# A pool of their own for the tiles of two matmul operands, in a two-layer decoder trunk

## The chip, the cores and the metric

One core of a Trainium2 chip runs the whole kernel. A time is that of one execution on the device, in microseconds (us); the runs shown are three, and their median is what a version is judged by. A profiled execution is a further one, with the hardware profiler on, and has a time of its own.

## The reference

The kernel computes two decoder layers on a residual stream x of 512 tokens by 1024 features, in float32. Each layer is a mixer and then a squared-ReLU MLP, with an RMS norm before each:

```python
for layer in range(DEPTH):                     # DEPTH = 2
    h = rmsnorm(x, norm_gains[layer, 0])
    if layer % 2 == 0:
        x = x + stick_breaking_mixer(h, ...)   # 16 heads of 64; w_qkv 1024x3072, w_o 1024x1024
    else:
        x = x + hgrn2_mixer(h, ...)            # 8 heads of 128; w_in 1024x4096, w_o 1024x1024
    h = rmsnorm(x, norm_gains[layer, 1])
    a = relu(h @ w1)                           # w1 1024x4096
    x = x + (a * a) @ w2                       # w2 4096x1024
```

The stick-breaking mixer is causal attention whose weights are products of sigmoids in place of a softmax, with normalised queries and keys. The HGRN2 mixer is a gated linear recurrence, done in blocks. Nearly all of the arithmetic is in the five matrix products with weights.

## The kernel before

The residual stream lies transposed in `xT`, eight tiles of 128 features by 512 tokens. Every product with weights is done in three passes, to keep the precision of float32 with the faster fp32r matmul: an operand is split into a high part, rounded to fp32r, and a low part, the rest; the product is then high x high + low x high + high x low. So each product of one 128x128 block of weights is a triple of matmuls.

**Weights.** They come in slabs (`slab_halves`, line 247): 512 KB twice by DMA into `wr`, then ScalarE copies to `wh` (line 263) and VectorE subtracts to `wl` (line 264). Two slabs are held, one in use and the next in preparation. A slab has 1024 rows by 256 columns, or 512 by 512 in the two projections.

**Activations.** `act_pair` (line 335) takes two tiles of 128 by 512, a high and a low one. With tag P these are the normalised inputs `xh` and `xl` of a sub-layer (`Norm.split`, line 354), 16 tiles for the eight feature blocks. With tag Q they are the second moving operand: `hh` and `hl` of the MLP's hidden layer (line 677), or `oh` and `ol` of a mixer's output (`split_out`, line 338), 16 tiles too.

**Two forms of product.** In `gemm_w` (line 312) a block of the slab is stationary and an activation tile moves, all 512 columns of it; eight triples make one output tile. It is used for w1 with P moving, for w2 and the projections with Q moving, and for q and f of the recurrence with P moving. In `gemm_x` (line 324) it is the other way round: a 128x128 block of P is stationary, and 256 columns of the slab move; q, k, v of the attention and i, g of the recurrence are made so. The very last output tile of the kernel is done in two halves of 256 tokens each (line 686).

**Order.** TensorE's instructions are in an order written out by hand: `line.run` (line 130) interleaves the long products with the short tasks of the attention heads, the recurrence and the norms, by costs and due times in `COST` and `LAG`. The other engines' order comes from the scheduler. An MLP is four rounds; each makes eight hidden tiles with w1 and adds eight partial outputs of w2 to `xT`.

**Places in memory.** Tiles come from pools: `cp` for constants and `xT`, `wp` for the slabs, `ap` for everything else, `pp` in PSUM. The function `sb` (line 90) takes all tiles of `ap`; a tile's tag says which buffers it shares, and `BUFS` how many of them there are. The pools lie in SBUF in the order in which they are opened, from the lowest address up, behind 16 KiB that are reserved; within a pool the tags lie in the order of their first use. `cp` takes 22.4 KiB of each partition, `wp` 44 KiB (two `wh` and two `wl` of 8 KiB, three `wr` of 4), and `ap` the rest. In `ap`, the tags in their order and in KiB are AT 6, sq 4, R4 16, ss 0.25, P 32, st 0.75, sn 4, mqk 0.25, mx and rx 0.1, B 8, qT 26, X5 10, Q 32, bc 2, tf 0.1. The last address in use is 144 bytes under the end of the 224 KiB.

Of the kernel before, what the change touches and what calls it, by code (L numbers as in the profile page):

```python
# [58 lines left out]
def trunk(  # L59
# [18 lines left out]
    PSUM = bass.MemoryType.PSUM  # L78
    cp = ctx.enter_context(tc.tile_pool(name="cp", bufs=1))
    wp = ctx.enter_context(tc.tile_pool(name="wp", bufs=2))  # L80
    ap = ctx.enter_context(tc.tile_pool(name="ap", bufs=2))
    pp = ctx.enter_context(tc.tile_pool(name="pp", bufs=2, space=PSUM))

    BUFS = {
        "P": 16, "Q": 16, "X5": 2, "R4": 4, "B": 2, "qT": 13, "sn": 2, "AT": 3, "sq": 2, "bc": 1,
        "st": 6, "mx": 2, "rx": 2, "ss": 2, "mqk": 2, "tf": 4,
    }
    PB = {"mm": 2, "z": 2, "tr": 3, "av": 1}

    def sb(tag, shape=(P, S), dt=F32, name=None):  # L90
        return ap.tile(list(shape), dt, tag=tag, bufs=BUFS[tag], name=name or tag)

    def ps(tag, shape=(P, S), name=None):
        return pp.tile(list(shape), F32, tag=tag, bufs=PB[tag], name=name or f"ps_{tag}")
# [72 lines left out]
    nc.scalar.copy(ones_r, ones)  # L167

    rows = sb("AT", (40, P), name="rows")
    nc.sync.dma_start(out=rows[0:32, :], in_=norm_gains.rearrange("l j (k p) -> (l j k) p", p=P))  # L170
    nc.sync.dma_start(out=rows[32:40, :], in_=hg_lb_logits.rearrange("a (k p) -> (a k) p", p=P))
    warm = sb("sq", (P, 1), name="warm")
    nc.scalar.activation(out=warm, in_=ones[:, 0:1], func=AF.Sigmoid)
    cols = cp.tile([P, 40], F32, name="cols")
# [25 lines left out]
    def late_constants():  # L200
        nc.vector.tensor_mul(gqk, gq, gk)
        masks_i = sb("R4", (P, level_masks.shape[1]), I32, name="masks_i")
        nc.gpsimd.dma_start(out=masks_i, in_=level_masks)
        nc.gpsimd.tensor_copy(pairs, masks_i[:, 0 : P // 2])
        nc.gpsimd.tensor_copy(masks, masks_i[:, P // 2 :])

        lg = cols[:, 32:40]
        e0 = sb("st", (P, 32), name="e0")[:, :KT]  # L210
        e1 = sb("st", (P, 32), name="e1")[:, :KT]
        nc.vector.tensor_sub(lb, lg, lg)
        nc.scalar.activation(out=e0, in_=lb, func=AF.Sigmoid)
        nc.scalar.activation(out=e1, in_=lb, func=AF.Sigmoid, scale=-1.0)
        nc.vector.reciprocal(out=e1, in_=e1)
        nc.vector.tensor_mul(e0, e0, e1)
        nc.vector.reciprocal(out=e1, in_=e0)
        nc.vector.tensor_mul(e0, e0, e1)
        nc.vector.tensor_sub(lb, e0, e0)
        nc.vector.tensor_scalar(  # L220
            out=oml, in0=lb, scalar1=-1.0, scalar2=1.0, op0=ALU.mult, op1=ALU.add
        )
# [863 lines left out]
```

## Time and profile before

| | us |
|---|---|
| median of 3 runs | 1322.77 |
| lowest, highest | 1321.46, 1326.64 |
| profiled execution, its own time | 1325.41 |
| its span, first to last instruction | 1323.7 |
| TensorE busy (PE) | 1300.2 |
| VectorE busy (DVE) | 798.7 |
| ScalarE busy (ACT) | 446.0 |
| GpSimd busy (POOL) | 80.0 |

In the profile, PE is a matmul and PEld the load of its stationary operand, which goes beside it. Matmuls are pipelined: the end of one lies after the start of the next, and a busy PE is not a PE at its peak. The distance from start to start is what one costs. The mean granted clock of TensorE was 0.996 of its full speed. In the rows, an operand list such as `ps_mm<-xh,wh` has the moving operand first and the stationary one second; buffer numbers are left out.

### The profile page before, as it was taken

The page shows a single profiled execution, that of the slowest core. Times are in us where ns is not written, and L with a number is a line of the kernel's source. Part 1 is how long each engine was busy: PE and PEld are TensorE (multiplying, and loading weights), DVE is VectorE, ACT ScalarE, POOL GpSimd, SP SyncE. Part 2 cuts the span into 40 slices and gives each one's busy share as a digit, 9 for nine tenths or more (in the row PEclk, how much of TensorE's full clock was granted, in tenths as well). Part 3 has the DMA queues.
Part 4 walks back from the last instruction along what each step waited for, and adds up shares of the span by engine and source line. Part 5 has one row for each costly group of instructions (what it writes and reads, how often), then busy time and mean ns, then how long its engine had stood idle before and what let it go on. Part 6 is the DMA issues. An engine that isn't in the chain of part 4 may idle for free.

```text
span 1323.7 us, 17619 instructions
## 1 busy us (share of the span) xinstructions
PE 1300.2 (98%) x6993; PEld 1104.2 (83%) x6993; DVE 798.7 (60%) x1534; ACT 446.0 (34%) x756; POOL 80.0 (6%) x139
## 2 busy tenths in 40 slices
PE   7999999999999999999999999999999999999998
PEld 7989898778888888888888888888888888888887
DVE  5787687867535435345578888797764353453441
ACT  5554454544212222123333333342432221221221
POOL 0100000000000000000013222232000000000000
PEclk8999999999999999999999999999999999999999
DMA  5312121113333333333321222221333333333331
GB/s 178 108 33 65 33 68 61 49 48 96 96 96 96 96 96 96 96 96 96 96 89 47 88 64 65 64 65 64 96 96 96 96 96 96 95 96 94 97 96 48
DMA packets 110657, 110.64 MB, mean 84 GB/s; under 512 B 3848, under 2 KB 106416, under 8 KB 110576
## 3 DMA queue, kind: packets, MB, share of 16 engines
q1 hardware_dynamic: 110496, 109.22, 26.7%
q8 instruction: 55, 0.90, 0.3%
q0 software_dynamic: 80, 0.31, 0.1%
q14 instruction: 26, 0.21, 0.0%
HBM read 107.41 MB, written 2.10 MB: 83 GB/s over the span
## 4 chain that ended last, share of the span: by engine, by line
PE 84%; DVE 10%; POOL 2%; issue 2%; ACT 1%; SPq 1%; DMA 1%; DVEq 0%; POOLq 0%; ACTq 0%
PE ps_mm L151 70%; PE po L151 3%; PE ps_z L151 3%; POOL tot L812 2%; DVE sc L845 2%; PE ps_s L151 2%; DVE wl L264 2%; PE pa L155 1%; PE z L151 1%; DVE qr L826 1%; PE po_h L151 1%; PE ps_tr L151 1%; DVE sn L591 1%; DVE X L863 1%; DVE X L867 1%
## 5 line engine op out<-in xcount | busy, mean ns | idle before, releaser
L263 ACT CAST wh<-wr 128x1024 fp32r<-128x1024 f32 x198 | 199.8, 1051 | 399.8 <-PE ps_mm L151 367.8
L264 DVE TENSOR_TENSOR wl<-wr,wh 128x1024 fp32r<-128x1024 f32 x198 | 237.7, 1230 | 17.6 <-ACT wh L263 16.8
L151 PE MATMUL ps_mm<-xh,wh 128*128 128x512 f32 x592 | 232.1, 392 | 0.0
L151 PE MATMUL ps_mm<-xh,wl 128*128 128x512 f32 x592 | 230.5, 389 | 0.0
L151 PE MATMUL ps_mm<-xl,wh 128*128 128x512 f32 x592 | 230.5, 389 | 0.0
L151 PE MATMUL ps_mm<-hh,wh 128*128 128x512 f32 (+1 forms) x520 | 204.1, 393 | 0.0
L151 PE MATMUL ps_mm<-hh,wl 128*128 128x512 f32 (+1 forms) x520 | 203.6, 392 | 0.0
L151 PE MATMUL ps_mm<-hl,wh 128*128 128x512 f32 (+1 forms) x520 | 203.5, 391 | 0.0
L151 PE MATMUL ps_mm<-wh,xh 128*128 128x256 f32 x592 | 173.6, 293 | 0.0
L695 DVE TENSOR_TENSOR xT<-xT,ps_mm 128x512 f32<-128x512 f32 x63 | 43.4, 688 | 213.2 <-PE ps_mm L151 213.2
L151 PE MATMUL ps_mm<-wl,xh 128*128 128x256 f32 x592 | 167.8, 283 | 3.1 <-DVE wl L459 3.1
L151 PE MATMUL ps_mm<-wh,xl 128*128 128x256 f32 x592 | 167.6, 283 | 0.0
L151 PEld LDWEIGHTS ps_mm<-xh,wl 128*128 128x128 f32 x592 | 111.1, 188 | 23.2
L151 PEld LDWEIGHTS ps_mm<-xh,wh 128*128 128x128 f32 x592 | 111.2, 188 | 22.7
L151 PEld LDWEIGHTS ps_mm<-xl,wh 128*128 128x128 f32 x592 | 111.2, 188 | 22.5
L151 PEld LDWEIGHTS ps_mm<-wh,xh 128*128 128x128 f32 x592 | 113.5, 192 | 4.2 <-issue 3.6
L151 PEld LDWEIGHTS ps_mm<-wl,xh 128*128 128x128 f32 x592 | 113.6, 192 | 3.9 <-DVE wl L459 3.3
L151 PEld LDWEIGHTS ps_mm<-hh,wl 128*128 128x128 f32 x520 | 97.6, 188 | 22.9
L151 PEld LDWEIGHTS ps_mm<-hl,wh 128*128 128x128 f32 x520 | 97.7, 188 | 22.7
L151 PEld LDWEIGHTS ps_mm<-hh,wh 128*128 128x128 f32 x520 | 97.7, 188 | 22.6
L672 DVE SCALAR_TENSOR_TENSOR u<-ps_mm,R 128x512 f32<-128x512 f32 x60 | 41.5, 692 | 123.1 <-PE ps_mm L151 123.1
L151 PEld LDWEIGHTS ps_mm<-wh,xl 128*128 128x128 f32 x592 | 113.5, 192 | 0.0
(213 smaller groups left out, 1653.6 us busy)
## 6 DMA issues: line engine op xcount, KB each, us to landing
wr<-in_mlp_w_dram SPq DMA_DIRECT2D x128, 512.0 KB, 3.7
wr<-in_hg_w_in_dram SPq DMA_DIRECT2D x32, 512.0 KB, 3.8
wr<-in_sb_w_qkv_dram SPq DMA_DIRECT2D x22, 512.0 KB, 3.5
wr<-in_sb_w_o_dram SPq DMA_DIRECT2D x8, 512.0 KB, 3.9
wr<-in_hg_w_o_dram SPq DMA_DIRECT2D x8, 512.0 KB, 3.7
xin<-in_x_dram SPq DMA_DIRECT2D x8, 256.0 KB, 5.3
out_dram<-o SPq DMA_DIRECT2D x7, 256.0 KB, 2.3
wr<-in_sb_w_qkv_dram SPq DMA_DIRECT2D x4, 256.0 KB, 5.5
```

Source lines behind the costliest of these rows:

```text
L151: nc.tensor.matmul(o, lhsT=lhsT, rhs=rhs, start=start, stop=stop, **kw)
L155: nc.tensor.transpose(o, in_, ident)
L263: nc.scalar.copy(hi[:, c, :], raw)
L264: nc.vector.tensor_tensor(out=lo[:, c, :], in0=raw, in1=f(hi[:, c, :]), op=ALU.subtract)
L591: nc.vector.tensor_tensor_scan(out=rev, data0=rev, data1=later[:, S - W :][:, ::-1], initial=1.0, op0=ALU.mult, op1=ALU.max,)
L672: nc.vector.scalar_tensor_tensor(out=u, in0=p, scalar=0.0, in1=norm.R, op0=ALU.max, op1=ALU.mult)
L695: nc.vector.tensor_add(xT[m], xT[m], p)
L812: nc.gpsimd.tensor_tensor(out=tots[H][:, :, None], in0=t0, in1=t1, op=ALU.mult)
L826: nc.vector.tensor_tensor(out=q1, in0=q1, in1=t0.to_broadcast([P, S // (2 * H), H]), op=ALU.mult)
L845: nc.vector.copy_predicated(out=o, mask=mask.rearrange("p (g w) -> p g w", g=g)[:, None].to_broadcast([P, 2, g, w]), data=data.rearrange(" ...
L863: nc.vector.tensor_tensor(out=o, in0=qv[:, :, :, part * H : part * H + w], in1=tv[:, :, :, part - 1, None].to_broadcast([P, TT, g, w]), op ...
L867: nc.vector.tensor_tensor(out=C, in0=B[:, :, :, H:], in1=tv[:, :, :, 1, None].to_broadcast([P, TT, g, wc]), op=ALU.mult,)
```

## The change

A pool `gp` is opened between the slabs' pool and `ap`. Tiles with the tags P and Q come from it, each with its 16 buffers as before; all others stay in `ap`.

```diff
     cp = ctx.enter_context(tc.tile_pool(name="cp", bufs=1))
     wp = ctx.enter_context(tc.tile_pool(name="wp", bufs=2))
+    gp = ctx.enter_context(tc.tile_pool(name="gp", bufs=16))
     ap = ctx.enter_context(tc.tile_pool(name="ap", bufs=2))
...
     def sb(tag, shape=(P, S), dt=F32, name=None):
-        return ap.tile(list(shape), dt, tag=tag, bufs=BUFS[tag], name=name or tag)
+        pool = gp if tag in "PQ" else ap
+        return pool.tile(list(shape), dt, tag=tag, bufs=BUFS[tag], name=name or tag)
```

No other tag is a part of the text "PQ", so no other tile is moved to `gp`. The tiles of `ap` that lay behind P or Q, or before them, get other addresses too.

## Rows read from the trace of the kernel before

**Rows 1.** Page, part 1: busy us, share of the span, instructions of each engine.
```profile
PE 1300.2 (98%) x6993; PEld 1104.2 (83%) x6993; DVE 798.7 (60%) x1534; ACT 446.0 (34%) x756; POOL 80.0 (6%) x139
```
**Rows 2.** Page, part 4: the chain that ended last, by engine, by line.
```profile
PE 84%; DVE 10%; POOL 2%; issue 2%; ACT 1%; SPq 1%; DMA 1%; DVEq 0%; POOLq 0%; ACTq 0%
PE ps_mm L151 70%; PE po L151 3%; PE ps_z L151 3%; POOL tot L812 2%; DVE sc L845 2%; PE ps_s L151 2%; DVE wl L264 2%; PE pa L155 1%; PE z L151 1%; DVE qr L826 1%; PE po_h L151 1%; PE ps_tr L151 1%; DVE sn L591 1%; DVE X L863 1%; DVE X L867 1%
```
**Rows 3.** The same chain in order of time: start us, us, what.
```profile
321.86 342.41 PE ps_mm L151 x1488
...
973.96 306.71 PE ps_mm L151 x1335
```
**Rows 4.** Tiles xh, hh, oh on TensorE, one stretch each: duration ns, first and last start.
```profile
L151 PE MATMUL ps_mm<-xh,wh x64: 389/389/393, 399.1 to 442.0; 128*128 128x512 f32 x64
...
L151 PE MATMUL ps_mm<-hh,wh x64: 392/394/398, 442.7 to 486.8; 128*128 128x512 f32 x64
...
L151 PE MATMUL ps_mm<-oh,wl x32: 392/395/398, 287.5 to 309.2; 128*128 128x512 f32 x32
```
**Rows 5.** Timeline of TensorE, two short stretches: start us, us, instruction.
```profile
520.11 0.39 PE L151 MATMUL ps_mm<-xh,wh 128*128 128x512 f32 x1
520.34 0.39 PE L151 MATMUL ps_mm<-xl,wh 128*128 128x512 f32 x1
520.56 0.39 PE L151 MATMUL ps_mm<-xh,wl 128*128 128x512 f32 x1
...
521.47 0.39 PE L151 MATMUL ps_mm<-xh,wh 128*128 128x512 f32 x1
...
553.15 0.39 PE L151 MATMUL ps_mm<-hh,wl 128*128 128x512 f32 x1
553.38 0.40 PE L151 MATMUL ps_mm<-hh,wh 128*128 128x512 f32 x1
553.62 0.39 PE L151 MATMUL ps_mm<-hl,wh 128*128 128x512 f32 x1
553.85 0.40 PE L151 MATMUL ps_mm<-hh,wl 128*128 128x512 f32 x1
...
554.55 0.39 PE L151 MATMUL ps_mm<-hh,wl 128*128 128x512 f32 x1
...
553.15 0.19 PEld L151 LDWEIGHTS ps_mm<-hh,wh 128*128 128x128 f32 x1
553.38 0.19 PEld L151 LDWEIGHTS ps_mm<-hl,wh 128*128 128x128 f32 x1
```
**Rows 6.** Windows, w1 and w2: busy us of PE, PEld, DVE, ACT, POOL, PEclk, DMA.
```profile
400.00:442.00 42.00, 42.00 (x187) 34.76 (x187) 21.88 (x30) 11.23 (x15) 0.00 (x0) 1.00 0.33 101
443.00:487.40 44.40, 44.40 (x192) 35.73 (x191) 15.86 (x18) 8.17 (x9) 0.00 (x0) 1.00 0.30 95
```
**Rows 7.** Instruction groups by line, one of each three: count | busy us, mean ns.
```profile
L151 PE MATMUL ps_mm<-xh,wh 128*128 128x512 f32 x592 | 232.1, 392 | 0.0
...
L151 PE MATMUL ps_mm<-hh,wh 128*128 128x512 f32 (+1 forms) x520 | 204.1, 393 | 0.0
...
L151 PE MATMUL ps_mm<-wh,xh 128*128 128x256 f32 x592 | 173.6, 293 | 0.0
...
L151 PE MATMUL ps_mm<-ol,wh 128*128 128x512 f32 x128 | 50.9, 398 | 0.0
...
L151 PE MATMUL ps_z<-xh,wh 128*128 128x512 f32 x48 | 19.0, 396 | 0.0
```
**Rows 8.** 256 columns moving: tile wl at the start, then the timeline's end.
```profile
L151 PE MATMUL ps_tr<-wl,xh x32: 283/283/283, 29.5 to 40.7; 128*128 128x256 f32 x32
...
1313.13 0.29 PE L151 MATMUL ps_mm<-hh,wh 128*128 128x256 f32 x1
...
1313.86 0.28 PE L151 MATMUL ps_mm<-hh,wh 128*128 128x256 f32 x1
```
**Rows 9.** Instruction groups by line: matmuls with other moving tiles that get new places.
```profile
L151 PE MATMUL po<-at,V 128*64 128x128 f32 x320 | 48.9, 284 | 1.2 <-DVE at L610 1.2
...
L151 PE MATMUL ps_s<-X,kk 128*128 128x196 f32 (+1 forms) x192 | 40.9, 342 | 7.7 <-DVE sc L845 6.7 <-DVE sc L888 0.9
...
L151 PE MATMUL z<-kst,qh 128*128 128x256 f32 (+1 forms) x64 | 23.5, 368 | 3.2 <-ACT sg L589 3.2
```
**Rows 10.** Tiles hl and xT on VectorE: duration ns least, median, most.
```profile
L679 DVE TENSOR_TENSOR hl<-a,hh x64: 691/693/695, 326.2 to 1275.2; 128x512 fp32r<-128x512 f32 x64
...
L695 DVE TENSOR_TENSOR xT<-xT,ps_mm x63: 686/689/690, 360.1 to 1313.3; 128x512 f32<-128x512 f32 x63
```

## The prediction

> **What bounds the kernel now.** I read the busy shares first [rows 1]: TensorE is busy for 98% of the span, VectorE for 60%, ScalarE for 34%. Then the chain of waits by engine and line [rows 2]: 84% of it is TensorE, and 70% of the span is one line, the matmuls into `ps_mm`. In order of time [rows 3] this chain has two pieces of 342.41 and 306.71 us with nothing but such matmuls in them, 1488 and 1335 in a row. No other engine and no DMA ends a wait there. What the kernel takes in these stretches is a number of matmuls times the spacing from the start of one to the start of the next, so I looked at the spacing.
>
> It is not the same everywhere, and this is the finding on which all else rests. All long matmuls have 512 columns, a 128x128 stationary block of a slab (`wh` or `wl`), and one of two kinds of moving operand: tag P (`xh`, `xl`: w1, and q and f of the recurrence) or tag Q (`hh`, `hl`: w2; `oh`, `ol`: the projections). With P moving, 64 triples start from 399.1 to 442.0 us: 42.9/63/3 = 227.0 ns each [rows 4]. With Q moving, 64 triples start from 442.7 to 486.8 us: 44.1/63/3 = 233.3 ns [rows 4]. The timeline has the same at close range [rows 5]: seven starts with P from 520.11 to 521.47 are 1.36/6 = 226.7 ns apart, seven with Q from 553.15 to 554.55 are 1.40/6 = 233.3. The starts with P are 0.22 or 0.23 us apart, those with Q 0.23 and 0.24 in turn. The projection, which reads Q against slabs of another row length, has 32 triples from 287.5 to 309.2 us [rows 4]: 21.7/31/3 = 233.3. So the spacing goes with the tag, not with the slab's layout. Nor does it go with the load around it: in the w1 stretch VectorE is busy 21.88 us of 42.00 and the DMAs move 101 GB/s, in the w2 stretch 15.86 of 44.40 and 95, with a granted clock of 1.00 (2.4 GHz) in both [rows 6]. The less loaded stretch is the slower one.
>
> **Where the tiles lie.** The pools stand one behind the other in the order in which they are opened, the tags within a pool in the order of first use. In the program of before, the slabs take 38.4 to 82.4 KiB of each partition. In `ap`, 26.2 KiB of other tags (AT 6, sq 4, R4 16, ss 0.25) come ahead of P, which has 108.6 to 140.6 KiB; then come 49.1 KiB (st, sn, mqk, mx, rx, B, qT, X5), and Q has 189.75 to 221.75. So the slow tag is the one that lies last. After the change P has 82.4 to 114.4 and Q 114.4 to 146.4: Q moves into the stretch in which P now runs at 227 ns (they overlap by 26 of 32 KiB), and P moves 26.2 KiB down. What lay between goes up by 64 or 32 KiB; R and acc stay.
>
> **The change part by part.** No instruction is added or removed; each tag keeps its number of buffers, so no wait changes its partner, and the order on the queues is as it was. Only addresses change. The terms:
>
> *Q as the moving operand.* The spacing falls from 233.3 to that of P, between 226.7 and 227.0, so by 6.3 to 6.6 ns; I take 6.5. Counts [rows 7]: `hh` and `hl` 3 x 520 = 1560, less the last tile's two halves with 256 columns (48), which leaves 1512; `oh` and `ol` 3 x 128 = 384. Together 1896 x 6.5 ns = 12.3 us. All of it is on the path, since the chain there is TensorE alone. From both sides: nothing, if the spacing doesn't hang on the place; at the other end, if lying near the slabs did more than P shows, the smallest step between two starts in [rows 5], 0.22 us for all, is 1896 x 13.3 = 25.2 us.
>
> *P as the moving operand.* 3 x 592 + 3 x 48 = 1920 matmuls [rows 7]. I take 0, since P is at the fast spacing already. Bounds: down to 0.22 us is a gain of 1920 x 6.8 = 13.1 us; up to what Q shows now is a loss of 1920 x 6.5 = 12.5 us.
>
> *P as the stationary operand* (256 columns of slab moving, 1776 in `ps_mm` alone [rows 7]). These start (40.7 - 29.5)/31/3 = 120.4 ns apart [rows 8]. In the last tile, where Q is moving with 256 columns, seven starts from 1313.13 to 1313.86 are 121.7 ns apart [rows 8]. With half the columns the two places thus differ by 1.3 ns and not by half of 6.5, so I take 0; bounds 1776 x 1.3 = 2.3 us either way.
>
> *The tiles that go up:* `X` (192 matmul records), `at` (320), `kst` (2 x 64) as moving operands [rows 9]. Most have 128 to 256 columns, so with the 1.3 ns of [rows 8] the upper bound is 640 x 1.3 = 0.8 us; I take 0.
>
> *VectorE and ScalarE:* 512 columns take VectorE 693 ns where Q is written (`hl`) and 689 where only xT is, at 22 to 38 KiB [rows 10]. Their times hardly know the place. I take 0; the 4 ns between them on 64 instructions would be 0.3 us, beside TensorE's work.
>
> What is late next, once w2 goes faster: a slab must be ready each 48 matmuls, after 10.9 us in place of 11.2. The w1 stretch already runs at this rate without a wait [rows 4, 6], with more work on VectorE in it. So nothing new comes to the path.
>
> Sum: 1325.41 us (the profiled execution, its span 1323.7 within) - 12.3 = 1313.1. The median of the runs is 2.64 us under that execution, so 1322.77 - 12.3 = **1310.5 us**, 0.9% less.
>
> The 1272 triples with 512 columns of [rows 7] show two spacings for one form of instruction [rows 5]. The Trainium skill speaks against any of this: "TensorE: Matmul & The Clock Gate", part 2 on what happens when you issue a matmul, gives TensorE two independent read ports, so that loading the next weights takes no bandwidth from the running matmul, and "SBUF — State Buffer", section Who interferes with whom, says that PE never waits on anyone. By these pages the place of a tile is worth nothing, and the sum would be 1322.8. The trace disagrees as far as both groups can't be at the same cost: 227.0 and 233.3 ns, which these pages give no ground for.
>
> **The rivals.**
>
> *Nothing happens: 1322.8 us.* Then the 6.5 ns belong to something else that goes with Q, say which tile follows which. For it: the profile shows no addresses, and P and Q differ in other things too, as the tiles of a pair are handed out in another order. Against it: `hh` and `oh` are written by different code and read in different stages against different slabs, and have the same 233.3 ns.
>
> *It is the position relative to the slab, and P loses: 1335.3 us.* While a matmul streams its tile, the weights of the next are read from a slab ([rows 5]: loads and matmuls alternate at the same starts). If what counts is how the two addresses stand to one another within a short period, distance means nothing. In the program of before, P begins 128 bytes past a multiple of 512, Q 256 past, the slabs 384 past. P and slab are thus 256 apart in that period, Q and slab 128. After the change all three stand at 384, with no distance at all, in a relation that no long matmul of before has. If that relation costs what Q's does, Q gains nothing and P loses: 1920 x 6.5 = 12.5 us, 1322.77 + 12.5 = 1335.3. For it: a regular alternation of 0.23 and 0.24 us, as of two readers in step [rows 5]. Against it: were the period 256 bytes or less, the new relation would be the one that P has now, which is the fast one. It decides from the point where both tags share a spacing of over (1920 x 226.8 + 1896 x 233.3)/3816 = 230.0 ns.
>
> *Nearer is faster still: about 1284 us,* all long matmuls at 0.22 us: 13.1 + 25.2 = 38.3 us. Against it: the whole of P, over 32 KiB, has one spacing, with no slope.
>
> **How the numbers follow.** Forecast (Q takes P's spacing, own range 1306 to 1315 us by 1 ns on 1896 matmuls and the bounds of the small terms): 0.62. Nothing: 0.14. Relative position with a loss: 0.18. Nearer still: 0.06. What this kernel's measurement can tell from no change is about 0.5%, 6.6 us: faster 0.68, same 0.14, slower 0.18. The range of 1302 to 1330 us leaves out the last rival and most of the losing one, which fills 1325 to 1342.
>
> **What would show it.** In the changed kernel's trace, 64 triples with `hh` moving should go from first to last start in 42.9 us instead of 44.1, those with `xh` in the same 42.9; 32 triples with `oh` in 21.1 instead of 21.7. The alternation of 0.23 and 0.24 us should be gone. The instruction counts should be the same on each engine. If `xh` takes 44.1 us, the relative position it was; if `hh` stays at 44.1 with `xh` at 42.9, the place is without effect. A wait of TensorE for `wl` inside the two long pieces would show the cover of the slabs gone.

## The result and the profile after

| | before | after |
|---|---|---|
| median of 4 runs, us | 1322.32 | 1311.97 |
| lowest, highest, us | 1321.46, 1326.64 | 1310.3, 1314.0 |
| profiled execution, us | 1325.41 | 1314.0 |
| its span, us | 1323.7 | 1312.3 |

The changed kernel takes 0.9916 of the time before (95% interval 0.9889 to 0.9942): 10.35 us less by the medians, 11.4 by the two profiled spans. Run once more on another chip, beside the kernel before, it was 1311.48 against 1323.28 us, 0.991 (0.9893 to 0.9926), 11.8 less. The forecast was 1310.5. One execution of e2_p256 (2133.62 us) and one of e7_64_160 (3623.22 us), each far slower than the others of its kernel, are left out of the medians below.

All lines of the changed kernel stand two lower than before (L151 is now L153). The page's part 1, busy time of each engine, answers to [rows 1]:

```profile
PE 1288.4 (98%) x6993; PEld 1103.6 (84%) x6993; DVE 798.1 (61%) x1534; ACT 446.0 (34%) x756; POOL 79.7 (6%) x139
```

The counts of instructions are those of before on every engine, and only TensorE's busy time has moved by more than 0.6 us, by 11.8. The chain that ended last, in order of time (start us, us, what), answers to [rows 3]; the first and the third line are the two mixers' projections:

```profile
287.09 21.98 PE ps_mm L153 x96
321.35 337.28 PE ps_mm L153 x1488
...
927.65 27.23 PE ps_mm L153 x120
...
967.16 302.60 PE ps_mm L153 x1335
```

The two long pieces hold the same numbers of matmuls as in [rows 3], 1488 and 1335, and are 5.13 and 4.11 us shorter. The two projection pieces took 22.59 and 27.89 us before, so they gave 0.61 and 0.66. Together 10.5 of the 11.4 us; 0.5 of the rest lies behind the second long piece, where the last w2 matmuls stand in short pieces of the chain.

Tiles xh, hh and oh on TensorE in the same stretches as in [rows 4] (durations in ns, first to last start in us):

```profile
L153 PE MATMUL ps_mm<-xh,wh x63: 389/389/389, 398.0 to 440.2; 128*128 128x512 f32 x63
...
L153 PE MATMUL ps_mm<-hh,wh x64: 389/389/389, 440.9 to 483.7; 128*128 128x512 f32 x64
...
L153 PE MATMUL ps_mm<-oh,wh x32: 389/389/499, 287.0 to 308.2; 128*128 128x512 f32 x32
```

With hh moving, 64 triples go from first to last start in 42.8 us, which is 42.8/63/3 = 226.5 ns a matmul where it was 233.3. With xh moving it is 42.2/62/3 = 226.9 (227.0 before); with oh 21.2/31/3 = 228.0 (233.3 before). The timeline has it at close range (start us, us, instruction), for [rows 5]:

```profile
553.07 0.39 PE L153 MATMUL ps_mm<-hh,wh 128*128 128x512 f32 x1
553.29 0.39 PE L153 MATMUL ps_mm<-hl,wh 128*128 128x512 f32 x1
553.52 0.39 PE L153 MATMUL ps_mm<-hh,wl 128*128 128x512 f32 x1
...
554.43 0.39 PE L153 MATMUL ps_mm<-hh,wh 128*128 128x512 f32 x1
```

Seven starts in 1.36 us: 226.7 ns, by steps of 0.22 and 0.23 as P has them. The alternation of 0.23 and 0.24 is gone. Two windows, of w1 and of w2 (length, then busy us of PE, PEld, DVE, ACT, POOL, the granted clock, the DMA share, GB/s), for [rows 6]:

```profile
400.00:440.00 40.00, 40.00 (x179) 33.10 (x178) 20.26 (x28) 10.13 (x13) 0.00 (x0) 1.00 0.33 106
443.00:483.00 40.00, 40.00 (x178) 33.13 (x177) 14.21 (x17) 6.39 (x7) 0.00 (x0) 1.00 0.34 105
```

In 40 us w1 and w2 now start as many matmuls, 179 and 178, at the same granted clock of 1.00 (2.4 GHz) and under the same DMA load. Before, the 44.40 us of w2 held 192, which is 173 in 40 us [rows 6].

The terms costed at nothing: 256 columns of slab moving (tile xh at the start, then hl on VectorE), for [rows 8, 10]; the groups of other moving tiles that got new places (count | busy us, mean ns | idle before), for [rows 9]:

```profile
L153 PE MATMUL ps_tr<-wl,xh x32: 283/283/283, 29.0 to 40.1; 128*128 128x256 f32 x32
...
L681 DVE TENSOR_TENSOR hl<-a,hh x64: 691/693/694, 325.7 to 1264.5; 128x512 fp32r<-128x512 f32 x64
```

```profile
L153 PE MATMUL po<-at,V 128*64 128x128 f32 x320 | 48.9, 283 | 1.1 <-DVE at L612 1.1
...
L153 PE MATMUL ps_s<-X,kk 128*128 128x196 f32 (+1 forms) x192 | 40.9, 342 | 7.5 <-DVE sc L847 6.6 <-DVE sc L890 0.5
...
L153 PE MATMUL z<-kst,qh 128*128 128x256 f32 (+1 forms) x64 | 23.8, 372 | 3.1 <-ACT sg L591 3.1
```

All stand within a per cent or so of before: (40.1 - 29.0)/31/3 = 119.4 ns for 120.4, 693 ns for 693, 48.9 and 40.9 us unchanged, 23.8 for 23.5.

### The profile page after: what moved, and what is told of

Its sections match the earlier page's. It is cut to its first block, busy times and chain, and to the rows that moved or that the text cites. A ratio compares the mean times of both kernels' runs of the same rounds, so it can differ in the third digit from the quotient of the medians.

```text
span 1312.3 us, 17619 instructions
## 1 busy us (share of the span) xinstructions
PE 1288.4 (98%) x6993; PEld 1103.6 (84%) x6993; DVE 798.1 (61%) x1534; ACT 446.0 (34%) x756; POOL 79.7 (6%) x139
## 4 chain that ended last, share of the span: by engine, by line
PE 83%; DVE 10%; issue 2%; POOL 2%; ACT 1%; SPq 1%; DMA 0%; DVEq 0%; POOLq 0%; ACTq 0%
PE ps_mm L153 70%; PE po L153 3%; PE ps_z L153 3%; POOL tot L814 2%; DVE sc L847 2%; DVE wl L266 2%; PE ps_s L153 2%; PE pa L157 1%; PE z L153 1%; DVE qr L828 1%; PE po_h L153 1%; DVE sn L593 1%; DVE X L865 1%; DVE X L869 1%; DVE ql L565 1%
## 5 line engine op out<-in xcount | busy, mean ns | idle before, releaser
L153 PE MATMUL ps_mm<-xh,wh 128*128 128x512 f32 x592 | 232.1, 392 | 0.0
L153 PE MATMUL ps_mm<-xh,wl 128*128 128x512 f32 x592 | 230.5, 389 | 0.0
L153 PE MATMUL ps_mm<-xl,wh 128*128 128x512 f32 x592 | 230.4, 389 | 0.0
L153 PE MATMUL ps_mm<-hh,wh 128*128 128x512 f32 (+1 forms) x520 | 201.3, 387 | 0.0
L153 PE MATMUL ps_mm<-hh,wl 128*128 128x512 f32 (+1 forms) x520 | 200.7, 386 | 0.0
L153 PE MATMUL ps_mm<-hl,wh 128*128 128x512 f32 (+1 forms) x520 | 200.6, 386 | 0.0
L153 PE MATMUL ps_mm<-wh,xh 128*128 128x256 f32 x592 | 173.3, 293 | 0.0
L153 PE MATMUL ps_mm<-wl,xh 128*128 128x256 f32 x592 | 167.7, 283 | 3.8 <-DVE wl L461 3.3
L153 PE MATMUL ps_mm<-wh,xl 128*128 128x256 f32 x592 | 167.5, 283 | 0.0
L153 PEld LDWEIGHTS ps_mm<-xh,wl 128*128 128x128 f32 x592 | 111.1, 188 | 23.1
L153 PEld LDWEIGHTS ps_mm<-xl,wh 128*128 128x128 f32 x592 | 111.2, 188 | 22.6
L153 PEld LDWEIGHTS ps_mm<-xh,wh 128*128 128x128 f32 x592 | 111.2, 188 | 22.5
L153 PEld LDWEIGHTS ps_mm<-wl,xh 128*128 128x128 f32 x592 | 113.4, 192 | 4.8 <-DVE wl L461 3.5
L153 PEld LDWEIGHTS ps_mm<-wh,xh 128*128 128x128 f32 x592 | 113.2, 191 | 4.2 <-issue 3.6
L674 DVE SCALAR_TENSOR_TENSOR u<-ps_mm,R 128x512 f32<-128x512 f32 x60 | 41.5, 691 | 123.1 <-PE ps_mm L153 123.1
L153 PEld LDWEIGHTS ps_mm<-hl,wh 128*128 128x128 f32 x520 | 97.7, 188 | 19.6
L153 PEld LDWEIGHTS ps_mm<-hh,wl 128*128 128x128 f32 x520 | 97.7, 188 | 19.6
L153 PEld LDWEIGHTS ps_mm<-hh,wh 128*128 128x128 f32 x520 | 97.7, 188 | 19.5
L153 PEld LDWEIGHTS ps_mm<-wh,xl 128*128 128x128 f32 x592 | 113.4, 192 | 0.0
```

Source lines behind the costliest of these rows:

```text
L153: nc.tensor.matmul(o, lhsT=lhsT, rhs=rhs, start=start, stop=stop, **kw)
L674: nc.vector.scalar_tensor_tensor(out=u, in0=p, scalar=0.0, in1=norm.R, op0=ALU.max, op1=ALU.mult)
```

## The experiments

Every experiment leaves the arithmetic and the number of matmuls as they are and moves tiles in SBUF. A small spacer does it: the tags mx and rx are 64 bytes each, `pad` is 32 or 64, and a tag takes its place in its pool by its first use. I call *relation* the start of a moving tile less the start of a slab's buffer, modulo 256 bytes. All tiles of P and Q are 2 KiB and all rows of a slab are multiples of 512 bytes, so within a tag the relation is one number. Before, P has 0 (281 x 256 bytes behind the first `wh`) and Q 128 (605.5 x 256); in the changed kernel both have 0. So this change altered two things at once, Q's place and Q's relation. Everything else, P included, moved by a multiple of 256 bytes or not at all: modulo 256 only Q has moved.

The results in one table. The spacing is (last - first start)/(n - 1)/3 of the rows with `wh` stationary from about 400 to 480 us, in ns; the place is that of P's and Q's first byte in KiB. Each ratio is to the kernel before as it ran on the same chip: its median was 1322.62 us beside e1 to e4, 1324.32 beside e5 to e8 and 1322.82 beside e9. The ratio is estimated over all the executions, so it need not be the quotient of two medians.

| kernel | relation P, Q | place P, Q | median us | ratio to before (95%) | spacing P, Q |
|---|---|---|---|---|---|
| before | 0, 128 | 108.6, 189.75 | 1322.32 | 1 | 227.0, 233.3 |
| changed | 0, 0 | 82.4, 114.4 | 1311.97 | 0.9916 (0.9889 to 0.9942) | 226.9, 226.5 |
| e1_q128 | 0, 0 | 108.6, 189.6 | 1313.48 | 0.9929 (0.9912 to 0.9947) | 227.2, 226.8 |
| e2_p256 | 128, 128 | 108.8, 189.75 | 1330.56 | 1.006 (1.0041 to 1.0079) | 232.7, 232.1 |
| e3_last | 0, 0 | 159.9, 191.9 | 1312.13 | 0.9926 (0.9905 to 0.9947) | 226.7, 226.5 |
| e4_near | 128, 128 | 82.5, 114.8 | 1331.67 | 1.0071 (1.0052 to 1.009) | 232.7, 232.1 |
| e5_all0 | 0, 0 | 82.5, 114.5 | 1311.60 | 0.991 (0.9893 to 0.9926) | 226.2, 226.9 |
| e6_32_96 | 32, 96 | 82.4, 114.5 | 1334.12 | 1.0073 (1.0058 to 1.0088) | 233.3, 233.3 |
| e7_64_160 | 64, 160 | 82.4, 114.5 | 1330.06 | 1.0044 (1.0028 to 1.0061) | 228.7, 233.9 |
| e8_192_224 | 192, 224 | 82.6, 114.6 | 1331.78 | 1.0061 (1.0046 to 1.0076) | 233.3, 233.3 |
| e9_split | 128 to wh, 0 to wl | 82.5, 114.5 | 1335.62 | 1.0095 (1.0079 to 1.0111) | 233.3, 233.3 |

**Place or relation.** Four kernels cross the two. The first leaves Q at its far place and moves it down by 128 bytes: the tags mx and rx, which lay ahead of Q, go to a pool behind `ap`.

```diff
     ap = ctx.enter_context(tc.tile_pool(name="ap", bufs=2))
+    zp = ctx.enter_context(tc.tile_pool(name="zp", bufs=2))
...
-        return ap.tile(list(shape), dt, tag=tag, bufs=BUFS[tag], name=name or tag)
+        pool = zp if tag in ("mx", "rx") else ap
+        return pool.tile(list(shape), dt, tag=tag, bufs=BUFS[tag], name=name or tag)
```

> The kernel before with one edit: the tags mx and rx (128 bytes together) go to a pool behind ap. Q then begins 128 bytes lower, still at the far end (189.6 KiB), and stands 128 past a multiple of 512, as P does in the kernel before; P and the slabs stay where they were. If the place decides (Q slow because it lies far up), nothing changes: 233.3 ns from start to start with hh or oh moving, 1322 us. If it is the position relative to the slab within 512 bytes, Q gets P's spacing, 226.7 ns, where it lies: 1896 x 6.5 ns = 12.3 us less, about 1310 us.

Tiles xh and hh on TensorE in e1_q128:

```profile
L153 PE MATMUL ps_mm<-xh,wh x50: 389/389/389, 404.2 to 437.6; 128*128 128x512 f32 x50
...
L153 PE MATMUL ps_mm<-hh,wh x62: 389/389/389, 438.2 to 479.7; 128*128 128x512 f32 x62
```

Q is fast at 189.6 KiB: 41.5/61/3 = 226.8 ns. These 128 bytes alone give 9.1 us of the 10.35 (1322.62 to 1313.48), and the interval holds the ratio of the whole change. That speaks against the place.

The second does the opposite to the kernel before: mx and rx are used first of all, so they lie ahead of P, and P moves up by 128 bytes.

```diff
+    for t in ("mx", "rx"):
+        nc.gpsimd.memset(sb(t, (P, TT), name="pre"), 0.0)
     rows = sb("AT", (40, P), name="rows")
```

> The kernel before with mx and rx used once at the start (two small memsets on GpSimd), so that they lie ahead of P: P begins 128 bytes higher, at 108.8 KiB, and stands 256 past a multiple of 512, as Q does; Q stays where it was. If the place decides: P keeps 226.7 ns, Q 233.3, 1322 us. If the relative position decides: P is slowed to 233.3 ns where it lies, 1920 x 6.5 ns = 12.5 us more, about 1335 us.

Tiles xh and hh in e2_p256, then the timeline with xh moving:

```profile
L151 PE MATMUL ps_mm<-xh,wh x51: 390/393/404, 404.7 to 439.6; 128*128 128x512 f32 x51
...
L151 PE MATMUL ps_mm<-hh,wh x57: 390/393/404, 440.3 to 479.3; 128*128 128x512 f32 x57
```

```profile
410.78 0.40 PE L151 MATMUL ps_mm<-xh,wl 128*128 128x512 f32 x1
411.01 0.40 PE L151 MATMUL ps_mm<-xh,wh 128*128 128x512 f32 x1
411.26 0.40 PE L151 MATMUL ps_mm<-xl,wh 128*128 128x512 f32 x1
```

P, fast in [rows 4], becomes slow in nearly its old place: 34.9/50/3 = 232.7 ns, with steps of 0.23 and 0.25 us, and the kernel 7.9 us slower than before. Less than the 12.5 us expected, and the trace shows why. Over all steps with xh or xl moving the mean rises from 227.0 to 232.3 ns, 5.3 and not 6.5. Q, which lies where it lay, falls from 233.2 to 232.4, and the matmuls with the slab moving fall from 119.6 to 118.9. On 1920, 1896 and 1821 of them that is 10.2 - 1.5 - 1.3 = 7.4 us. So the spacing at relation 128 is not one number: hh at the same address shows steps of 229 and 238 ns in turn in the kernel before, and irregular ones of 228 to 241 here. Why is open.

The third and the fourth do the same with the changed kernel: e3_last opens the new pool behind `ap`, so that both tags lie far up with relation 0; e4_near keeps the near place and gives both 128.

```diff
e3_last
+    ap = ctx.enter_context(tc.tile_pool(name="ap", bufs=2))
     gp = ctx.enter_context(tc.tile_pool(name="gp", bufs=16))
-    ap = ctx.enter_context(tc.tile_pool(name="ap", bufs=2))
e4_near
-        pool = gp if tag in "PQ" else ap
+        pool = gp if tag in ("P", "Q", "mx", "rx", "mqk") else ap
...
+    for t in ("mx", "rx"):
+        nc.gpsimd.memset(sb(t, (P, TT), name="pre"), 0.0)
```

> The changed kernel with the new pool opened behind ap instead of behind the slabs' pool: P at 159.9 to 191.9 KiB, Q at 191.9 to 223.9, as far from the slabs as can be; both still stand 384 past a multiple of 512, as the slabs do. If the place decides: Q at 233.3 ns, and P too for those of its tiles that lie beyond the limit, 1324 to 1337 us. If the relative position decides: both at 226.7 ns, 1312 us, the same as the changed kernel.

> The changed kernel with small tags in the new pool: mx and rx ahead of P, mqk between P and Q. P is at 82.5 KiB and stands 0 past a multiple of 512, Q at 114.8 KiB and stands 256 past; the slabs stay at 384. If the place decides: both at 226.7 ns, 1312 us. If the relative position decides: Q is back at 233.3 ns, 12.3 us more, though it lies next to P; and P takes the spacing of a relation not yet seen (half of 512 plus 128 from the slab, the mirror of Q's), somewhere between 224 and 238 ns: 1319 to 1346 us in all.

Tiles xh and hh, first in e3_last, then in e4_near:

```profile
L153 PE MATMUL ps_mm<-xh,wh x56: 389/389/389, 404.8 to 442.2; 128*128 128x512 f32 x56
...
L153 PE MATMUL ps_mm<-hh,wh x55: 389/389/389, 442.9 to 479.6; 128*128 128x512 f32 x55
```

```profile
L153 PE MATMUL ps_mm<-xh,wh x53: 390/393/404, 404.2 to 440.5; 128*128 128x512 f32 x53
...
L153 PE MATMUL ps_mm<-hh,wh x56: 390/393/404, 441.2 to 479.5; 128*128 128x512 f32 x56
```

Far with relation 0 is fast (1312.13 us, the changed kernel's time), near with 128 is slow (1331.67). With these the place is out, for the places tried: the spacing follows the 128 bytes, in both tags, near and far. What e1 adds besides: its Q stands 256 bytes off the slab modulo 512, as P did before, and is as fast as at 0 modulo 512; so 256 bytes are a whole period.

**To one another, or to a line of memory?** In all of these the slabs stood still. e5_all0 puts 128 bytes ahead of the slabs, so that slabs, P and Q all move by 128.

```diff
     cp = ctx.enter_context(tc.tile_pool(name="cp", bufs=1))
+    hp_ = ctx.enter_context(tc.tile_pool(name="hp", bufs=2))
...
-        pool = gp if tag in "PQ" else ap
+        pool = gp if tag in "PQ" else hp_ if tag in ("mx", "rx") else ap
```

> The changed kernel with mx and rx (128 bytes) in a pool ahead of the slabs: slabs, P and Q all move up by 128 bytes and all stand 0 past a multiple of 512. If what counts is how the moving tile stands to the slab (theory now), they stand alike, so both keep 226.7 ns and the time is 1312 us. If it is the moving tile's own address (a multiple of 256 is slow, 128 past one is fast), both go to 232.4 to 233.3 ns: 3816 x 6 ns = 23 us more, 1335 us.

```profile
L154 PE MATMUL ps_mm<-xh,wh x48: 388/389/390, 404.6 to 436.5; 128*128 128x512 f32 x48
...
L154 PE MATMUL ps_mm<-hh,wh x63: 388/389/390, 437.2 to 479.4; 128*128 128x512 f32 x63
```

Both are fast (the fence is of tiles xh and hh in e5_all0), at 1311.60 us. What counts is how the two operands stand to one another.

Nor is it the work of other engines on the same memory. In the trace of before, 770 of the steps with hh or hl moving have no instruction of VectorE, ScalarE or GpSimd running in them; their mean is 233.3 ns, that of the 723 others 233.2. And the DMAs move 105 GB/s in the fast w2 stretch of the changed kernel, 95 in the slow one of before [rows 6].

**Between 0 and 256.** Three kernels with other spacers, each with a relation of its own for P and for Q. In e6_32_96 there are 32 bytes of pad ahead of P and mx between P and Q; in e7_64_160 mx ahead, rx and 32 bytes of pad between; in e8_192_224 mx, rx and 64 bytes of pad ahead, 32 of pad between. The edit of e6_32_96, to which the two others are alike:

```diff
-        pool = gp if tag in "PQ" else ap
+        pool = gp if tag in ("P", "Q", "mx") else ap
...
+    pad = gp.tile([P, 8], F32, tag="pad", bufs=1, name="pad")
+    nc.gpsimd.memset(pad, 0.0)
```

> The changed kernel with spacers in the new pool: P begins 32 bytes further than the slabs' position within 256, Q 96 further. Seen so far: 0 is fast (226.7 ns), 128 slow (232.4 or 233.3). If the cost falls with the distance from 128 by steps, P (32) is at 227 to 228 and Q (96) at 230 to 233: 1317 to 1326 us. If only equal positions are fast, both are at 232 to 233: 1332 to 1336. If only the one at 128 is slow, both stay at 226.7: 1312.

> As the run before, P 64 bytes further than the slabs' position within 256, Q 160. Falling by steps from 128: P near 229 to 230 ns, Q near 230 to 233, 1322 to 1330 us. Only equal positions fast: 1332 to 1336. Only 128 slow: 1312.

> As the two runs before, P 192 bytes further than the slabs' position within 256, Q 224. Falling by steps from 128: P near 229 to 230 ns, Q at 227 to 228, 1315 to 1321 us. Only equal positions fast: 1332 to 1336. Only 128 slow: 1312. Should one of these six offsets fall below 226.7 ns, it points to a better version.

Tiles xh and hh in e6_32_96, then in e7_64_160, then in e8_192_224:

```profile
L153 PE MATMUL ps_mm<-xh,wh x52: 393/396/398, 404.1 to 439.8; 128*128 128x512 f32 x52
...
L153 PE MATMUL ps_mm<-hh,wh x57: 394/399/400, 440.5 to 479.7; 128*128 128x512 f32 x57
```

```profile
L153 PE MATMUL ps_mm<-xh,wh x51: 391/392/393, 404.8 to 439.1; 128*128 128x512 f32 x51
...
L153 PE MATMUL ps_mm<-hh,wh x58: 392/397/401, 439.8 to 479.8; 128*128 128x512 f32 x58
```

```profile
L153 PE MATMUL ps_mm<-xh,wh x51: 393/394/399, 404.2 to 439.2; 128*128 128x512 f32 x51
...
L153 PE MATMUL ps_mm<-hh,wh x58: 394/396/399, 439.9 to 479.8; 128*128 128x512 f32 x58
```

No slope from 0 to 128 and back: relations 32, 96, 160, 192 and 224 have all 233 to 234 ns. 64 is the least slow, 34.3/50/3 = 228.7 in this stretch and 230.9 over all steps with xh or xl moving. Of the eight relations in the table only 0 is fast, and the times of 1330 to 1334 us are those of both tags slow. So the second outcome expected, only equal positions fast, is the one that came, with 64 as a milder case.

**Which of the two reads.** While a matmul streams its tile, the next block of the slab is loaded [rows 5]. A pass over a triple takes `wh`, `wh` and `wl`. e9_split puts 128 bytes between the buffers of `wh` and those of `wl`, so that the tiles have relation 0 to one and 128 to the other. If the block loaded meanwhile decided, or the matmul's own block, one or two of a triple would be slow and the rest fast.

```diff
-        pool = gp if tag in "PQ" else ap
+        pool = gp if tag in "PQ" else wp if tag in ("mx", "rx") else ap
...
+    wh0 = wp.tile([P, KT, SLAB], F32R, tag="wh", bufs=2, name="wh")
+    for t in ('mx', 'rx'):
+        nc.gpsimd.memset(sb(t, (P, TT), name="pre"), 0.0)
...
-        "w": [wp.tile([P, KT, SLAB], F32R, tag=t, bufs=2, name=t) for t in ("wh", "wl")],
+        "w": [wh0, wp.tile([P, KT, SLAB], F32R, tag="wl", bufs=2, name="wl")],
```

> The changed kernel with 128 bytes (mx and rx) between the wh and the wl buffers: P and Q stand as wl does within 256 bytes, and 128 away from wh. In a triple, wh is loaded while the third matmul (xh,wl) and the first (xh,wh) run, wl while the second (xl,wh) runs. If the moving tile's relation to the block that is being loaded for the next matmul decides, only the second matmul of each triple is fast: from its start to the next 226 to 228 ns, the other two 230 to 240; two of 1272 x 3 matmuls in three slow, 2544 x 6 ns = 15 us more, about 1327 us. If the relation to the block that the matmul itself uses decides, the third (xh,wl) is the fast one, at the same time. If both tags must stand right to all of the slab, all three are slow: 1335 us.

The timeline of e9_split with xh and xl moving:

```profile
401.87 0.39 PE L153 MATMUL ps_mm<-xh,wh 128*128 128x512 f32 x1
402.10 0.40 PE L153 MATMUL ps_mm<-xl,wh 128*128 128x512 f32 x1
402.33 0.40 PE L153 MATMUL ps_mm<-xh,wl 128*128 128x512 f32 x1
402.57 0.39 PE L153 MATMUL ps_mm<-xh,wh 128*128 128x512 f32 x1
402.80 0.40 PE L153 MATMUL ps_mm<-xl,wh 128*128 128x512 f32 x1
```

All three of a triple are slow: 0.70 us from `xh,wh` to `xh,wh`, 233.3 ns each, by steps of 0.23 and 0.24. By the means over all their steps `xh,wh` takes 232.5 ns, `xl,wh` 232.6 and `xh,wl` 234.9. So neither reading holds by itself: `wh` off relation 0 makes all three slow. Two things are not told apart here. The stationary buffers `wh` and `wl` now also stand 128 bytes off each other, and the mirror case, `wl` off and `wh` at 0, was not run. What happens inside stays open.

**A kernel from this.** With the slab moving (256 columns) and P stationary, 0 is the slowest relation. In e7_64_160 P has relation 64 to the slab, and in the stretch of [rows 8] its tile xh shows

```profile
L153 PE MATMUL ps_tr<-wh,xh x32: 275/277/277, 27.8 to 38.3; 128*128 128x256 f32 x32
```

which is 10.5/31/3 = 112.9 ns a matmul, against 119.4 in the changed kernel at relation 0. That stretch is the best one: over all its slab-moving steps the mean is 115.4 ns, where the changed kernel has 119.6, and steps of 113, 114, 117 and 118 ns are mixed. At 128 (e2_p256) it is 118.9, at 32 118.3, at 192 116.9. e10_both wants both: `wh` and `wl` of a slab in one buffer with 256 spare bytes, the slab 64 bytes into it where an activation is to move (relation 0) and at its start where the slab is to move (P less slab is 64).

```diff
+    def slab_tiles(kt, nc_, off):
+        n = kt * nc_
+        w = wp.tile([P, 2 * n + 64], F32R, tag="w", bufs=2, name="w")
+        return [
+            w[:, off + i * n : off + (i + 1) * n].rearrange("p (k c) -> p k c", c=nc_) for i in range(2)
+        ]
...
-        plan += [full(sb_w_qkv[0], 0, n * D + g * SLAB) for n in range(3)]
+        plan += [full(sb_w_qkv[0], 0, n * D + g * SLAB, 0) for n in range(3)]     # default: 16 (64 bytes)
...
-        plan += [full(hg_w_in[0], 0, n * D + hp * SLAB) for n in range(4)]
+        plan += [full(hg_w_in[0], 0, n * D + hp * SLAB, 0 if n > 1 else 16) for n in range(4)]
```

(Beside this, mx lies ahead of P, and the tile `ones` became a part of `before`.)

> The changed kernel with the slab placed by its use: wh and wl of a slab lie in one buffer with 256 bytes to spare (the room comes from dropping a tile of ones that another tile holds too); where the activations move, P and Q stand as the slab does within 256 bytes; where the slab moves, P stands 64 bytes further than the slab, the relation at which the slab-moving matmuls were fastest (117.8 ns against 120.0, run e7_64_160). If the relation decides for both kinds, the 512-column matmuls keep 226.7 to 227.1 ns and the 256-column ones lose 2 to 4 ns each on 1823: 4 to 8 us less than the changed kernel, 1304 to 1308 us. If the waits of the attention stage for VectorE and ScalarE take it up again, 1309 to 1312.

It took 1308.96 us, 0.9892 (0.9876 to 0.9909) of before, just under the second outcome expected, in which waits take the gain up. The 512-column matmuls of the MLP stay fast (means of 226.8 and 226.9 ns). The mean step with the slab moving falls from 119.6 to 116.2 ns, and all these steps added up (those under 0.3 us) from 224.8 to 219.8 us, 5.0 less. TensorE's waits show where a part of that went (us in total, times, longest), in the changed kernel and in e10_both:

```profile
PE ps_s L153 <- DVE sc L847: 6.6, 16, 0.7
...
PE z L153 <- ACT sg L591: 3.1, 3, 1.1
...
PE ps_s L153 <- DVE sc L890: 0.5, 2, 0.4
```

```profile
PE ps_s L153 <- DVE sc L854: 8.0, 16, 0.8
PE z L153 <- ACT sg L598: 3.9, 3, 1.6
...
PE ps_s L153 <- DVE sc L897: 1.6, 4, 0.6
```

13.5 us instead of 10.2: in the mixers, where the slab moves, VectorE and ScalarE end waits, and the waits for them grew by 3.3 us. The two profiled spans, 1312.3 and 1310.1 us, differ by 2.2. To tell these, both ran again on one chip:

> The changed kernel unchanged, on the same chip as the next one, to hold the two against each other: 1310 to 1313 us, a ratio to the kernel before of 0.991 to 0.993.

> The kernel of run e10_both once more, beside the changed kernel on one chip. Its slab-moving matmuls took 222.2 us in that run against 227.6 in the changed kernel's trace, 5.4 us less, and waits on VectorE and ScalarE took part of that up again. If this is a gain of the whole: 1307 to 1309 us, 2 to 4 us under the changed kernel. If the 3 us of run e10_both were chance: the same time as the changed kernel within 1 us.

1311.48 us for the changed kernel, 0.991 (0.9893 to 0.9926), and 1309.84 for the other, 0.9903 (0.9885 to 0.9921). The intervals overlap: 1.6 us in its favour, which these runs can't tell from none. The traces of this pair say the same as those of the first: the slab-moving steps gave 8.2 us (226.0 to 217.8), the three waits grew by 4.0 (10.2 to 14.2), and the spans differ by 3.6 (1311.7 and 1308.1).

## Why the prediction was right, and where it was not

*The bound and the finding: right.* TensorE sets the end, two spacings stood in one form of instruction, and the slow one became the fast one. hh went to 42.8 us for 64 triples (forecast 42.9), xh stayed at 227 ns, oh's 32 triples took 21.2 (21.1), the alternation is gone, the counts are the same, and inside the two long pieces TensorE has no wait.

*The size: 12.3 us forecast, 10.35 and 11.8 by the two pairs of medians, 11.4 by the spans.* The spacing term was 6.5 ns on 1896 matmuls. The two long pieces gave 9.24 us on 1383 matmuls with Q, 6.7 each. What is short lies in the projections, where 384 matmuls were to give 2.5 us. The two pieces that hold 216 of them show 1.27, 5.9 each. The 168 others stand between tasks of the heads and the recurrence, and the piece of the first projection starts no earlier than before (287.09, before 286.97). So "All of it is on the path, since the chain there is TensorE alone" was too wide for these; that the waits there took up what they gained is argued, not shown.

*The cause: wrong.* The step that failed is the one from the tags to the place, "So the slow tag is the one that lies last", and with it "Q moves into the stretch in which P now runs at 227 ns" as the reason for the gain. The runs show the relation in its place: e1 and e3 are fast far up, e2 and e4 slow in P's own stretch or near the slabs. The relation to the slab is what decides (e5), and the mechanism is that of the losing rival, with a period of 256 bytes in place of 512. The prediction had the case in its sentence against that rival: "were the period 256 bytes or less, the new relation would be the one that P has now, which is the fast one". It gave this the weight of an objection, where it was an outcome of its own, with the same time as the forecast. The forecast's time came out right by luck, because both readings gave Q the spacing of P. With another 128 bytes in the new pool ahead of P, the reasoning by place would have said 1310 us; e4_near, which has them and a further 256 between P and Q, took 1331.67.

*"Nothing", for which the profile's lack of addresses spoke:* it fell with the result. What it said, that P and Q differ in other things than the place, was true: the relation was such a thing.

*"Nearer is faster still":* fell; no relation and no place had the steps of 0.22 us throughout that it wanted. The least is 226 to 227 ns, which at the granted 1.00 (2.4 GHz) is about 544 clocks for 512 columns, and the slow value of 233.3 about 560.

*The terms at nothing: right for this change.* Stationary P kept its relation to the slab (0 before and after), so its bound of 2.3 us was not touched; but the reasoning, that two places differ by only 1.3 ns there, would have missed what relation 64 gives, 4.2 ns in the mean and 6.5 in the best stretch. VectorE's 693 ns and the other moving operands stayed as forecast.

*The rule by which the place of a tile is worth nothing:* the distance is worth nothing indeed (e1, e3), but how the tile stands to the slab is worth 17.1 us between e2_p256 and e1_q128 on one chip. The Trainium skill's sentence in "SBUF — State Buffer", section Who interferes with whom, that PE never waits on anyone, and the independent read ports of the Trainium skill's "TensorE: Matmul & The Clock Gate", part 2, would give these two the same time. For the two operands of TensorE's own matmuls the measurement decides against that; what the ports do inside no run shows.

*What stays open:* which two reads meet, if it is reads that do, and why `wh` off relation 0 slows the whole triple (e9). No run isolates the pair outside this kernel, and no other element type and no other size of the blocks was tried.

## What to carry to other kernels

Where TensorE bounds a kernel, compare the start-to-start spacing of its matmuls by operand, not the busy share: 6.6 ns on half of the long ones was 0.9% here, with TensorE at 98% busy before and after. If one form shows two spacings, look at the addresses of moving and stationary operand modulo 256 bytes, and set them with spacers; any new small tile ahead of them can lose it again (1312 to 1332 us in e4_near). The best position depends on which operand moves: what is best for 512 columns of activation was the worst for 256 columns of slab. And a time that comes out as forecast shows no cause: a change of pool moves the place and the relation together, and it took kernels that vary one without the other to tell them apart.

## What the hardware showed that was not expected

- fp32r matmuls of 512 columns, each with a new stationary block, take 226.2 to 227.2 ns in the stretches of the table (228 in the projections) where moving and stationary tile begin at the same position modulo 256 bytes, and 228.7 to 233.9 at the other seven relations tried (32, 64, 96, 128, 160, 192, 224). The step is sharp: 32 bytes off costs as much as 128.
- With 256 columns, where the slab moves and P is stationary, it is the reverse. With P 0 bytes past the slab the mean step is 119.6 ns, at 128 it is 118.9, at 32 118.3, at 192 116.9 and at 64 115.4 (112.9 in its best stretch).
- The two buffers of a pair act together: with `wh` at 128 and `wl` at 0 all three matmuls of a triple take 232.5 to 234.9 ns (e9_split).
